# Half of q's projection ahead of the transposes of B's powers, q's convolution between the two rotations, and k's projection unsplit

## The chip, the cores and the metric

One core of a Trainium2 chip runs the whole kernel. The metric is the device time of one launch in microseconds, the median of the runs shown. A chance of "faster" or "slower" means by more than 0.3%.

## The reference

One layer of a decoder over 256 positions of width 1024, in float32. Cut to what matters here:

```python
h = rmsnorm(x, norm_mix_g)
p = h @ w_in            # [q | k | v | o (512 each) | i,f gates (4 each) | u (512)]
q, k = silu(conv4(q)), silu(conv4(k))          # causal, depthwise, 4 taps
A = sigmoid(o) * headnorm(mlstm(q, k, v, i, f))     # 4 heads of 128
s_t = a * s_(t-1) + Bbar u_t                   # S5: 32 groups of 16 channels, 64 complex states each
y = gelu(Re(C s) + D u);  z = y @ glu_w + glu_b;  B = z[:16] * sigmoid(z[16:])
x = x + concat([A, B]) @ w_out
x = x + top-1 of 4 expert groups, then top-2 of 8 SwiGLU experts (1024 -> 512 -> 1024) in it
return rmsnorm(x, norm_final_g)
```

## The kernel before

The program is one hand-written order of instructions for five in-order engines. There is no scheduler: what stands earlier in the code is issued earlier on its engine, and an instruction that waits holds everything behind it on that engine. SP is the queue of nearly all loads, and it is in order too.

**Memory.** `half(i)` is one of 23 buffers of 128 x 2048 float32 (1 MB each). They hold in turn the columns of w_in, temporaries, the split weights, w_out and at last the experts' weights. All 32 experts are streamed as 192 tiles of 1 MB; `fetch(upto)` issues tiles up to that number, and tile n goes into buffer `RO[n % 23]`. A tile's load waits until the last use of its buffer is over. Tiles 21 and 22 go into the buffers of `x1` (the residual) and of `xn`, which are free only when the parts of x for the experts have been made (lines 930 to 936).

**Front part, in the order of the code.** x is squared and transposed (L253 to L264), h = `h32` is written scaled and transposed (L277). `proj32T` (L422) multiplies w_in's columns with h in float32 and leaves the result transposed: u first, in PSUM banks 0 and 1. DVE meanwhile makes the powers of the S5 decay and B times those powers (`powers`, L355 to L363). u is copied to `U4`, C's transposes to `CT` (L477), the gates to `Gt` (L479). `transposeB` (L492, L495) turns B's powers; `inputs_to_states` (L520, L522) fills PSUM banks 4 to 7; `kernelK` and `transposeK` make the short S5 kernel, which ends in PSUM bank 1 and is read there by DVE at L596. Line 543 spreads rho, lines 544 to 546 make the sine and cosine (POOL made the angles, L391), lines 550 to 560 the gates' running sums. Then DVE runs `rotate(0)`, the kernel's mask (L595 to L598) and `rotate(1)` (L576 to L592): multiply by a rotation, scan, rotate back, for the two halves of the states.

**q, v, k, o.** q (L422, banks 2 and 3) and v (`proj32N`, L430, banks 0 and 1) run in float32. q then goes through `conv` (ACT L529, DVE L533, ACT L536). k and o are multiplied as sums of rounded parts: `prep` rounds a piece of a weight on ACT (L411) and subtracts it on POOL or DVE (L412), h is split the same way into `hH` and `hL` (L617, L618), and `projT` (L441 to L443) or `projN` (L453 to L457) takes three products. k also needs banks 2 and 3, so it starts only when q's convolution has read them. `states_to_outputs` (L648), `logweights` (L670) and the rest of k are interleaved; `outputs_back` (L655) turns S5's output, o follows, then k's convolution, `scores` (L664), the product with w_out in eight split pieces (`outs`, L805), the merge of the heads, and the routing. The experts (L1002) come last, in 16 pairs of 12 tiles.

The wait on PSUM that the change turns on stands in these lines of the order before:

```python
    rotate(1)
    run(proj32T("q", 2))
...
    run(proj32N("v", (0, 1)))
...
    for g in pc:
        run(g)
    cv = conv(0, 2)
```

## Time and profile before

| | |
|---|---|
| median of 3 runs | 642.94 us (642.47 to 644.63) |
| the profiled execution | 642.52 us, span 640.8 us |
| PE busy | 595.2 us (93% of the span) |
| DVE, ACT, POOL busy | 224.3, 135.5, 68.5 us |
| DMA, all queues | 219.78 MB, mean 343 GB/s |
| chain that ended last | PE 47%, DMA 32%, DVE 13%, ACT 4% |

Busy time is not the limit by itself: the chain names, going back from the end, what each piece of work waited for. The share of DMA comes from the stream of the experts; the shares of DVE and ACT come from the first 155 us. So the front has to be read engine by engine in time, and the experts' part by the rate of the stream.

### The profile page before, as it was taken

The numbers are of one execution on the slowest core, as the hardware profiler recorded it, in microseconds if no ns is written. First come the engines' busy times: TensorE is split into PE (matmuls) and PEld (weight loads), VectorE is DVE, ScalarE is ACT, GpSimd is POOL, SyncE is SP. The second block draws the span as 40 slices with busy tenths as digits, with TensorE's granted clock in tenths as the row PEclk, the third lists the DMA queues.
The fourth block names the chain that finished last, engine by engine and source line by source line (L and its number), as shares of the span: only waits on it lengthen the run. The fifth ranks groups of instructions, "written<-read, shape, count | busy, mean of one in ns | idle before, by whom it ended". The sixth has DMA issues, their size and how long they took to land.

```text
span 640.8 us, 8016 instructions
## 1 busy us (share of the span) xinstructions
PE 595.2 (93%) x3198; PEld 322.0 (50%) x3198; DVE 224.3 (35%) x548; ACT 135.5 (21%) x240; POOL 68.5 (11%) x77
## 2 busy tenths in 40 slices
PE   7979919999999999999999999999998999899993
PEld 6778408877864353353354335335343533354242
DVE  7939972186444231221212023122120212121123
ACT  2391364571332101101010010010100001001023
POOL 6010427255100000000000000000000000000003
PEclk8999958999999999999999999999999999999998
DMA  7781036657938999999999999999999999999992
GB/s 214 214 254 45 0 137 258 263 210 295 418 148 358 420 419 419 420 419 421 419 419 419 418 419 420 418 420 420 419 420 418 421 419 419 419 418 420 419 338 80
DMA packets 51336, 219.78 MB, mean 343 GB/s; under 512 B 15236, under 2 KB 20448, under 8 KB 27232
## 3 DMA queue, kind: packets, MB, share of 16 engines
q1 hardware_dynamic: 50944, 218.69, 85.4%
q8 instruction: 27, 0.44, 0.3%
q10 hardware_dynamic: 352, 0.54, 0.2%
q14 instruction: 13, 0.11, 0.0%
HBM read 218.17 MB, written 1.05 MB: 342 GB/s over the span
## 4 chain that ended last, share of the span: by engine, by line
PE 47%; DMA 32%; DVE 13%; ACT 4%; issue 1%; POOL 1%; SPq 0%; POOLq 0%; ACTq 0%; DVEq 0%
PE psum L1002 30%; DMA half<-in_expert_w_gate_dram 12%; DMA half<-in_expert_w_down_dram 9%; DMA half<-in_expert_w_up_dram 9%; PE psum L975 4%; PE psum L1017 3%; PE psum L805 2%; DVE mw L533 2%; PE psum L951 1%; DMA xs<-in_x_dram 1%; PE psum L648 1%; PE psum L441 1%; DVE half L583 1%; DVE half L357 1%; PE psum L1125 1%
## 5 line engine op out<-in xcount | busy, mean ns | idle before, releaser
L1002 PE MATMUL psum<-half,mw 128*64 128x512 f32 x1504 | 338.3, 596 | 9.5 <-DMA half<-in_expert_w_up_dram 4.2
L1002 PEld LDWEIGHTS psum<-half,mw 128*64 128x64 f32 x1504 | 110.3, 137 | 217.9 <-issue 186.9
L1009 DVE SCALAR_TENSOR_TENSOR Y<-psum,cst,Y 128x512 fp32r<-128x512 f32 x28 | 21.0, 751 | 134.2 <-ACT Y L1008 134.2
L1111 DVE TENSOR_TENSOR mw<-mw,psum 128x512 f32<-128x512 f32 x16 | 11.0, 687 | 143.7 <-PE psum L1002 143.7
L1008 ACT ACTIVATE Y<-psum,cst 128x512 fp32r<-128x512 f32 x28 | 19.2, 687 | 191.2 <-PE psum L1002 125.8
L1148 POOL MEMSET mw<- 128x2 f32 x1 | 0.1, 100 | 435.0 <-PE psum L1125 435.0
L412 POOL TENSOR_TENSOR half<-half,half 128x1024 fp32r<-128x1024 f32 x13 | 36.2, 2800 | 58.3 <-ACT half L411 47.6
L975 PE MATMUL psum<-cst,xs 128*128 128x256 bf16 (+1 forms) x384 | 40.9, 267 | 0.0
L975 PEld LDWEIGHTS <-xs 128*128 128x128 bf16 x384 | 40.0, 144 | 0.0
L1017 PE MATMUL psum<-Y,Sc 128*128 128x512 f32 x112 | 33.7, 423 | 0.0
L1126 ACT COPY mw<-psum 128x512 f32<-128x512 f32 x15 | 8.8, 587 | 114.4 <-PE psum L1125 114.4
L422 PE MATMUL psum<-half,half 128*128 128x256 f32 x128 | 30.8, 406 | 1.0 <-DVE half L277 1.0
L1017 PEld LDWEIGHTS psum<-Y,Sc 128*128 128x128 f32 x112 | 18.8, 188 | 25.3 <-issue 22.7
L958 DVE TENSOR_TENSOR mw<-psum,cst 128x512 f32<-128x512 f32 x32 | 22.1, 692 | 21.9 <-PE psum L975 18.3
L422 PEld LDWEIGHTS psum<-half,half 128*128 128x128 f32 x128 | 26.2, 206 | 5.2 <-DVE half L277 1.2
L805 PE MATMUL psum<-half,half 128*128 128x512 f32 x96 | 24.0, 401 | 0.6 <-ACT half L833 0.6
L441 PE MATMUL psum<-half,half 128*128 128x256 f32 x32 | 10.6, 332 | 14.2 <-DVE mw L533 14.0
L1104 ACT ACTIVATE mw<-psum 128x512 f32<-128x512 f32 x16 | 9.6, 597 | 52.8 <-PE psum L1002 52.8
L805 PEld LDWEIGHTS psum<-half,half 128*128 128x128 f32 x96 | 17.6, 188 | 4.7 <-ACT half L833 0.8
L992 DVE TENSOR_REDUCE cst<-psum 128x1 f32<-128x256 f32 x16 | 6.8, 425 | 26.9 <-PE psum L990 26.9
L411 ACT CAST half<-half 128x1024 fp32r<-128x1024 f32 x16 | 15.9, 1047 | 1.5 <-POOL half L412 1.0
L983 DVE TENSOR_SCALAR mw<-cst 128x64 f32<-128x64 f32 x64 | 15.6, 310 | 0.0
(348 smaller groups left out, 566.6 us busy)
## 6 DMA issues: line engine op xcount, KB each, us to landing
half<-in_expert_w_gate_dram SPq DMA_DIRECT2D x64, 1024.0 KB, 19.9
half<-in_expert_w_up_dram SPq DMA_DIRECT2D x64, 1024.0 KB, 19.9
half<-in_expert_w_down_dram SPq DMA_DIRECT2D x60, 1024.0 KB, 19.9
half<-in_w_in_dram SPq DMA_DIRECT2D x8, 1024.0 KB, 8.4
half<-in_w_out_dram SPq DMA_DIRECT2D x4, 1024.0 KB, 7.2
half<-in_expert_w_down_dram SPq DMA_DIRECT2D x6, 512.0 KB, 13.7
half<-in_w_in_dram SPq DMA_DIRECT2D x4, 512.0 KB, 7.3
xs<-in_x_dram SPq DMA_DIRECT2D x2, 512.0 KB
```

The costliest lines, as they stand in the source:

```text
L411: A.copy(made[i], w)
L412: es[i].tensor_tensor(rests[i], w, made[i].bitcast(F32), OP.subtract)
L422: MM(PS[:, bk + m // 2, 256 * (m % 2):256 * (m % 2) + 256], w[:, at:at + 128], flat(h32, c), start=c == 0 and m % 2 == 0, stop=c == 7, ski ...
L441: MM(o, wh[:, ms], flat(hH, c), start=c == 0 and m % 2 == 0, stop=False, skip_group_check=True)
L805: MM(PS[:, WB[2 * b + i], :], m[:, k % 4, ts], w[:, 512 * i:512 * i + 512], start=False, stop=n == 7 and m is ml, skip_group_check=True)
L958: TT(xg[:, cs, ss], PS[:, bk, :].rearrange("p (c s) -> p c s", c=n), fr(g2[:, cs], (1, n), (0, m)), OP.mult)
L975: MM(PS[:, DN[f % 2], m * c:m * c + m], xp[:, k, b, n * f + c::8], oh[:, b].rearrange("p e s -> p (e s)")[:, ss], start=c == b == k == 0, ...
L983: TS(ow[:, b, e], places, rk[:, b, 2 * pr + e:2 * pr + e + 1], wt[:, b, 2 * pr + e:2 * pr + e + 1], OP.is_equal, OP.mult)
L1002: MM(PS[64 * e:64 * e + 64, bk, 0:w[e].shape[-1]], lhs[:, c, 64 * e:64 * e + 64], w[e], start=c == 0, stop=c == n - 1, skip_group_check=True)
L1008: ACT(hi, src, AF.Copy, scale=w)
L1009: STT(lo, src, w, hi.bitcast(F32), OP.mult, OP.subtract)
L1017: MM(PS[:, WB[2 * b + n], :], Sc[:, b], Y[:, k], start=False, stop=False, skip_group_check=True)
```

## The change

Seven things change, all of them in order or in buffers except the second:

1. q's projection is a generator `qs`: four of its eight steps (16 products) run before `transposeB`, one between the two kernel transposes, three after. `conv(0, 2)` with its 12 DVE steps stands between `rotate(0)` and `rotate(1)`.
2. k is multiplied in float32 as q is (`proj32T("k", 2)`, 32 products) instead of in three rounded products; its four `prep` pieces are gone, `pieces` begins with o, and `projT` is gone.
3. h is rounded (`hH`) on ACT beside the first parameters, and `hL` is subtracted on POOL right behind the angles.
4. rho, the R rows and, ahead of B's copies, sine and cosine move earlier on ACT. In `transposeB` ACT takes one of four copies instead of two.
5. v's copy and C's powers follow v directly; the powers' temporaries move from buffers 21 and 17 to 0 and 1.
6. The loads of o and w_out move forward, `fetch` calls move back, and `RO` has a new order with buffer 22 for `xn` in place of 3.
7. The second half of x is loaded by ACT's queue, first of all; x's first square stands first on DVE; five small matmuls (`ident` with `ident`) stand between the transposes of x and u's projection.

The order table, the loads and the early part:

```diff
-    RO = (19, 17, 14, 16, 18, 11, 10, 20, 15, 22, 7, 21, 12, 2, 6, 0, 8, 1, 9, 4, 13, 5, 3)
+    RO = (14, 16, 18, 11, 10, 4, 19, 15, 7, 17, 20, 21, 12, 8, 1, 6, 0, 2, 3, 9, 13, 5, 22)
...
+    A.dma_start(xs[:, 1, :], xv[1])
...
-    SP.dma_start(xs[:, 1, :], xv[1])
...
+    STT(scr[:, 0, :], xs[:, 0, :], 1.0 / D, xs[:, 0, :], OP.mult, OP.mult, accum_out=ssq[:, 0:1])
+    V.tensor_copy(ldt0[0:16], rowsA[0:16, 0:2])
+    V.tensor_copy(rowsA[0:16, :].rearrange("p (g n) -> p g n", g=2), fr(ldt0[0:16], (1, 2), (0, 64)))
+    for b in range(2):
...
+        for c in range(8):
+            TR(xT[c][:, 128 * b:128 * b + 128], xs[:, b, c::8], ident)
...
+    for _ in range(2):
+        MM(PS[:, 0, 0:128], ident, ident, start=True, stop=True)
...
+    for _ in range(3):
+        MM(PS[:, 0, 0:128], ident, ident, start=True, stop=True)
...
+    hH, hL = [cuts(half(4 + i, F32R), (8, 2, 128))[0] for i in range(2)]
...
+    ACT(rho, b64(p["rho4"]), AF.Copy)
+    ACT(R[32:36], fr(dlt4[32:36], (0, 2), (1, 4), (0, 128)), AF.Copy)
...
+    for q in range(2):
+        A.copy(hH[:, 4 * q:4 * q + 4], h32[:, 4 * q:4 * q + 4])
...
-    t10, t11 = cuts(half(4), (4, 16, 16), (4, 16, 16))
+    t10, t11 = cuts(half(7), (4, 16, 16), (4, 16, 16))
...
-    pieces = [(g, i) for g in "ko" for i in range(4)] + [("w", k) for k in (4, 5, 6, 7, 0, 1, 2, 3)]
-    ROUNDED = (0, 2, 8, 20, 2, 6, 8, 9)
-    RESTS = (1, 3, 22, 9, 3, 0, 1, 4)
+    pieces = [(g, i) for g in "o" for i in range(4)] + [("w", k) for k in (4, 5, 6, 7, 0, 1, 2, 3)]
+    ROUNDED = (2, 9, 8, 1, 0, 3)
+    RESTS = (3, 19, 22, 6, 2, 9)
...
-    def projT(g, bk, i):
-        wh, wl = ready[g, i]
-        for cc in range(2):
-            c = 2 * i + cc
-            for m in range(4):
-                o = PS[:, bk + m // 2, 256 * (m % 2):256 * (m % 2) + 256]
-                ms = slice(512 * cc + 128 * m, 512 * cc + 128 * m + 128)
-                MM(o, wh[:, ms], flat(hH, c), start=c == 0 and m % 2 == 0, stop=False, skip_group_check=True)
-                MM(o, wh[:, ms], flat(hL, c), start=False, stop=False, skip_group_check=True)
-                MM(o, wl[:, ms], flat(hH, c), start=False, stop=c == 7, skip_group_check=True)
-                yield
...
+    qs = proj32T("q", 2)
...
+    for q in range(2):
+        cs = slice(4 * q, 4 * q + 4)
+        G.tensor_tensor(hL[:, cs], h32[:, cs], hH[:, cs].bitcast(F32), OP.subtract)
...
-            (A.copy if t % 2 else V.tensor_copy)(dst[:, 4 * t:4 * t + 4, :], src)
+            (A.copy if t == 3 else V.tensor_copy)(dst[:, 4 * t:4 * t + 4, :], src)
...
-    for i in range(2):
-        run(transposeB(i))
-    run(inputs_to_states())
...
-    ACT(rho, b64(p["rho4"]), AF.Copy)
...
+    STT(Bc[0:4], Gt[0:4], -1.0, Gt[0:4], OP.mult, OP.max)
+    for _ in range(4):
+        next(qs)
...
-    fetch(1)
...
+    load_w("o", (19, 21))
+    for i in range(2):
+        run(transposeB(i))
+    run(inputs_to_states())
...
+    next(qs)
     run(transposeK())
+    run(qs)
...
-    rotate(1)
-    run(proj32T("q", 2))
-    for j, a, b, n in ((0, 0, 96, 32), (1, 0, 64, 64), (2, 0, 32, 32), (2, 32, 64, 32), (2, 64, 96, 32), (3, 0, 0, 128)):
-        A.copy(Tz[b:b + n, :, j], KX[a:a + n])
-
-    run(proj32N("v", (0, 1)))
-    Cp = Bp
-    t10, t11 = cuts(half(17), (4, 16, 16), (4, 16, 16))
-    pc = [powers(V, Cp[0], CT, 1, True, 0, t00, t01), powers(V, Cp[1], CT, 1, True, 1, t10, t11)]
-    prep(2)
-    for g in pc:
-        run(g)
     cv = conv(0, 2)
     qk = cuts(half(7), (8, 256))[0]
     next(cv)
-    hH, hL = [cuts(half(4 + i, F32R), (8, 2, 128))[0] for i in range(2)]
-    for q in range(2):
-        cs = slice(4 * q, 4 * q + 4)
-        A.copy(hH[:, cs], h32[:, cs])
-        G.tensor_tensor(hL[:, cs], h32[:, cs], hH[:, cs].bitcast(F32), OP.subtract)
-    prep(4)
-    fetch(3)
+    for j, a, b, n in ((0, 0, 96, 32), (1, 0, 64, 64), (2, 0, 32, 32), (2, 32, 64, 32), (2, 64, 96, 32), (3, 0, 0, 128)):
+        A.copy(Tz[b:b + n, :, j], KX[a:a + n])
     for _ in range(4):
         next(cv)
-    V.memset(va[:, :, :, 128:129], 1.0)
+    prep(2)
+    rotate(1)
     next(cv)
+
+    run(proj32N("v", (0, 1)))
+    load_wo(4, 6)
     for b in range(2):
         A.copy(va[:, b, :, 0:128], PS[:, b, :].rearrange("p (h t) -> p h t", h=4))
-    load_w("o", (9, 6))
+    Cp = Bp
+    t00, t01 = cuts(half(0), (4, 16, 16), (4, 16, 16))
+    t10, t11 = cuts(half(1), (4, 16, 16), (4, 16, 16))
+    pc = [powers(V, Cp[0], CT, 1, True, 0, t00, t01), powers(V, Cp[1], CT, 1, True, 1, t10, t11)]
+    for g in pc:
+        run(g)
+    fetch(1)
+    load_wo(6, 0)
+    load_wo(2, 17)
+    prep(4)
...
+    run(proj32T("k", 2))
+    load_wo(0, 20)
+    states_to_outputs(0)
+    fetch(3)
...
-        run(projT("k", 2, i))
         logweights(i)
-        if i == 0:
-            states_to_outputs(0)
         TT(Em[:, i], PS[:, DB[i], :].rearrange("p (h t) -> p h t", h=4), fr(cap, (0, 4), (1, 128)), OP.min)
-    fetch(5)
...
-    fetch(7)
+    fetch(5)
...
-    for i in range(2, 4):
-        run(projT("k", 2, i))
...
-    load_wo(4, 0)
-    load_wo(6, 1)
...
-            prep(10)
...
-    load_wo(0, 4)
-    load_wo(2, 22)
...
+    fetch(8)
+    run(scores())
     fetch(9)
-    run(scores())
     for i in range(3):
         STT(Em[:, i], PS[:, (6, 4, 2)[i], :].rearrange("p (h t) -> p h t", h=4), 128.0 ** -0.5, Em[:, i], OP.mult, OP.mult)
+    prep(10, (G, V))
...
-    prep(14, (G, V))
-    prep(16, (G, V))
...
-    xn = cuts(half(3), (2, 1024))[0]
+    xn = cuts(half(22), (2, 1024))[0]
```

**PE, from u's projection to the first S5 output.** Buffers `half_5`, `half_6` are q's columns, `half_7`, `half_8` v's; `half_9`, `half_10` hold B's powers; `half_27`, `half_28` (before) are k's rounded parts and rests, `half_14`, `half_15` (after) k itself. In the order before, left of the S5 rows L520, L522 and L503:

```order
L463 MATMUL psum<-half_12_146,half_2_73 36x256 x8
L466 MATMUL psum<-ident,half_2_73 128x128 x8
L492 MATMUL psum<-ident,half_9_125 128x128 x16
L492 MATMUL psum<-ident,half_10_126 128x128 x16
...
L563 MATMUL psum<-ident,half_1_72 128x76
L512 MATMUL psum<-ident,mw 128x128 x4
L422 MATMUL psum<-half_12_146,half_5_104 128x256 x16
L422 MATMUL psum<-half_12_146,half_6_106 128x256 x16
L430 MATMUL psum<-half_7_118,half_12_146 128x512 x8
L430 MATMUL psum<-half_8_120,half_12_146 128x512 x8
L441 MATMUL psum<-half_30_631,half_27_610 128x256
L442 MATMUL psum<-half_31_632,half_27_610 128x256
```

And in the order of the change:

```order
L463 MATMUL psum<-ident,half_2_73 128x128 x8
L430 MATMUL psum<-half_12_144,half_5_104 128x256 x16
L491 MATMUL psum<-ident,half_9_125 128x128 x16
L491 MATMUL psum<-ident,half_10_126 128x128 x16
...
L430 MATMUL psum<-half_12_144,half_6_106 128x256 x4
L511 MATMUL psum<-ident,mw 128x128 x4
L430 MATMUL psum<-half_12_144,half_6_106 128x256 x12
L438 MATMUL psum<-half_7_118,half_12_144 128x512 x8
L438 MATMUL psum<-half_8_120,half_12_144 128x512 x8
L430 MATMUL psum<-half_12_144,half_14_212 128x256 x16
L430 MATMUL psum<-half_12_144,half_15_214 128x256 x16
L647 MATMUL psum<-half_13_204,half_18_220 64x128 x16
```

Half of q has moved ahead of the transposes of B's powers, and 32 products of k stand in a row where 96 rounded ones were spread among the S5 products.

**ACT, from the gates to the running sums.** `half_1_72` holds CT, `half_2_73` the gates. Before:

```order
L477 COPY half_1_72<-psum 64x256 x4
L479 ACTIVATE half_2_73<-psum,cst 36x256
L480 ACTIVATE mw<-cst 4x1024
L495 COPY half_21_385<-psum 128x512 x2
L495 COPY half_22_386<-psum 128x512 x2
L543 ACTIVATE half_20_286<-half_2_73 128x1024
L544 ACTIVATE half_19_285<-half_18_284 128x1024
L545 ACTIVATE half_18_284<-half_18_284 128x1024
L546 ACTIVATE half_19_285<-half_18_284,cst 128x1024
L551 ACT_TABLE_LOAD
```

In the change:

```order
L477 COPY half_1_72<-psum 64x256 x4
L479 ACTIVATE half_2_73<-psum,cst 36x256
L542 ACTIVATE half_22_297<-half_21_296 128x1024
L543 ACTIVATE half_21_296<-half_21_296 128x1024
L544 ACTIVATE half_22_297<-half_21_296,cst 128x1024
L494 COPY half_23_397<-psum 128x512
L494 COPY half_24_398<-psum 128x512
L551 ACT_TABLE_LOAD
```

The R rows and rho are gone from here, two copies have gone to DVE, and sine and cosine stand ahead of the copies.

**SP, behind k's columns.** In the change (`half_25`, `half_26` are o's columns, w_out's pieces are 4, 6, 2, 0 in this order):

```order
L173 DMA half_25_421<-in_w_in_dram 128x4x512
L173 DMA half_26_423<-in_w_in_dram 128x4x512
L180 DMA half_32_649<-in_w_out_dram 128x2x1024
L147 DMA half_35_665<-in_expert_w_gate_dram 128x2048
L180 DMA half_36_667<-in_w_out_dram 128x2x1024
L180 DMA half_37_669<-in_w_out_dram 128x2x1024
L180 DMA half_41_716<-in_w_out_dram 128x2x1024
L147 DMA half_42_734<-in_expert_w_gate_dram 128x2048
L147 DMA half_43_736<-in_expert_w_gate_dram 128x2048
L147 DMA half_46_789<-in_expert_w_gate_dram 128x2048
L147 DMA half_47_791<-in_expert_w_up_dram 128x2048
```

Before, three tiles of the experts stood ahead of o's columns and seven ahead of w_out; now one tile does.

## Rows read from the trace of the kernel before

**Rows 1.** windows of the late part: us, busy by engine (instructions), PEclk, DMA share, GB/s

```profile
118.00:153.00 35.00, 35.00 (x227) 28.43 (x226) 22.24 (x53) 19.85 (x41) 15.66 (x9) 1.00 0.56 214
...
184.00:195.00 11.00, 11.00 (x54) 3.82 (x55) 8.39 (x24) 8.45 (x14) 0.00 (x0) 1.00 0.29 96
...
195.00:614.00 419.00, 407.90 (x2050) 178.08 (x2046) 89.35 (x230) 38.56 (x61) 0.10 (x1) 1.00 1.01 418
```

**Rows 2.** timeline of DVE around the first experts: start, us, what

```profile
192.32 2.42 DVE L936 TENSOR_TENSOR xs<-half,xs 128x1024 bf16<-128x1024 f32 x2
```

**Rows 3.** PE's waits from 93 to 185 us: total, times, longest

```profile
PE psum L441 <- DVE mw L533: 14.0, 1, 14.0
...
PE psum L805 <- ACT half L833: 0.6, 1, 0.6
...
PE psum L829 <- DVE mw L794: 0.4, 1, 0.4
```

**Rows 4.** timeline of PE up to 120 us: start, us, what, [idle before]

```profile
12.17 16.84 PE L422 MATMUL psum<-half,half 128*128 128x256 f32 x64 [1.04 <-DVE half L277]
...
36.45 2.70 PE L492 MATMUL psum<-ident,half 128*128 128x128 f32 x20 [2.84 <-ACT half L477]
...
40.68 0.33 PE L520 MATMUL psum<-half,half 128*128 128x64 f32 x2
...
51.48 13.98 PE L422 MATMUL psum<-half,half 128*128 128x256 f32 x64
...
65.30 13.90 PE L430 MATMUL psum<-half,half 128*128 128x512 f32 x32
...
108.93 1.12 PE L670 MATMUL psum<-mw 36*128 36x512 f32 x2
...
110.19 1.97 PE L648 MATMUL psum<-half,half 128*64 128x128 f32 x32
...
118.03 1.95 PE L655 MATMUL psum<-ident,half 128*32 128x128 f32 x64
```

**Rows 5.** chain that ended last, up to 130 us: start, us, what

```profile
1.74 6.37 DMA xs<-in_x_dram
...
37.10 0.47 ACT half L479
...
41.49 1.06 ACT half L543
...
45.63 1.28 ACT L551
...
52.72 1.21 DVE mw L560
...
64.00 0.67 DVE half L596
```

**Rows 6.** timeline of POOL and DVE: two users of SBUF side by side

```profile
33.32 1.04 POOL L391 TENSOR_TENSOR half<-half,half 128x512 int32<-128x512 int32 x1
...
37.17 0.69 DVE L495 COPY half<-psum 128x512 f32<-128x512 f32 x1 [2.32 <-ACT half L477]
...
92.04 4.69 POOL L618 TENSOR_TENSOR half<-half,half 128x1024 fp32r<-128x1024 f32 x2 [13.47 <-ACT half L617]
...
97.00 2.34 DVE L634 TENSOR_SCALAR cst<-cst 128x4 f32<-128x4 f32 x1
```

**Rows 7.** timeline of ACT ahead of the S5 output

```profile
99.36 1.99 ACT L411 CAST half<-half 128x1024 fp32r<-128x1024 f32 x2 [0.96 <-POOL half L412]
...
110.09 0.60 ACT L685 ACTIVATE half<-psum 128x512 f32<-128x512 f32 x1 [7.43 <-PE psum L670]
...
110.64 1.15 ACT L688 ACTIVATE half<-half 128x512 f32<-128x512 f32 x2
```

**Rows 8.** timeline of DVE in the heads' norm

```profile
147.92 1.55 DVE L781 SCALAR_TENSOR_TENSOR cst<-mw 128x4 f32<-128x4 f32 x1
```

**Rows 9.** window in which PE stood behind v's projection

```profile
79.20:82.80 3.60, 0.00 (x0) 0.00 (x0) 3.57 (x6) 0.00 (x0) 0.00 (x0) 0.98 0.00 0
```

More of the change, by code (lines that the diff above doesn't have):

```diff
@@ L251, in tile_hymba @@
     flat = lambda t, c: t[:, c].rearrange("p b t -> p (b t)")
-    for c in range(8):
-        TR(xT[c][:, 0:128], xs[:, 0, c::8], ident)
-    TR(PS[:, 4, 0:48], rowsA[0:48, :], ident[0:48, 0:48])
-    for c in range(8):
-        TR(xT[c][:, 128:256], xs[:, 1, c::8], ident)
-    STT(scr[:, 0, :], xs[:, 0, :], 1.0 / D, xs[:, 0, :], OP.mult, OP.mult, accum_out=ssq[:, 0:1])
-    V.tensor_copy(rT, PS[:, 4, 0:48])
-    ldt, lre, lim = rT[:, 0:16], rT[:, 16:32], rT[:, 32:48]
+    STT(scr[:, 0, :], xs[:, 0, :], 1.0 / D, xs[:, 0, :], OP.mult, OP.mult, accum_out=ssq[:, 0:1])
[4 more added lines that the diff above has]
+            TR(xT[c][:, 128 * b:128 * b + 128], xs[:, b, c::8], ident)
+    TR(PS[:, 4, 0:48], rowsA[0:48, :], ident[0:48, 0:48])
+    for _ in range(2):
+        MM(PS[:, 0, 0:128], ident, ident, start=True, stop=True)
     STT(scr[:, 0, 0:512], xs[:, 1, 0:512], 1.0 / D, xs[:, 1, 0:512], OP.mult, OP.mult, accum_out=sh[:, 1, 0:1])
@@ L267, in tile_hymba @@
                   "cr", "ci", "t1", "t2", "rho4"], [spar[:, i] for i in range(20)]))
+    V.tensor_copy(rT, PS[:, 4, 0:48])
+    ldt, lre, lim = rT[:, 0:16], rT[:, 16:32], rT[:, 32:48]
     ACT(p["dt"], ldt, AF.Exp)
@@ L311, in tile_hymba @@
     ACT(p["rho4"], p["lrdt"], AF.Exp, scale=4.0)
+    U4, rho = cuts(half(18), (16, 64), (16, 64))
+    b64 = lambda ap: fr(ap, (1, 16), (0, 64))
+    ACT(rho, b64(p["rho4"]), AF.Copy)
+    ACT(R[32:36], fr(dlt4[32:36], (0, 2), (1, 4), (0, 128)), AF.Copy)
     rnd(V, p["n"], p["th"], 1.0 / TWO_PI)
@@ L382, in tile_hymba @@
     cosT, sinT = cuts(half(17), (16, 64), (16, 64))
-    U4, rho = cuts(half(18), (16, 64), (16, 64))
-    b64 = lambda ap: fr(ap, (1, 16), (0, 64))
     ta = ta.bitcast(I32)
@@ L479, in tile_hymba @@
     ACT(Gt[0:36], PS[0:36, 4, 0:256], AF.Identity, bias=gbias[0:36, 0:1])
-    ACT(R[32:36], fr(dlt4[32:36], (0, 2), (1, 4), (0, 128)), AF.Copy)
     cw = rTB[:, 0:32].rearrange("p (w t) -> p w t", w=4)
@@ L562, in tile_hymba @@
     A.copy(K4T, PS[:, 0, :])
-    TR(PS[:, 3, 0:76], rowsB[0:76, :], ident[0:76, 0:76])
-    A.copy(rTB[:, 0:76], PS[:, 3, 0:76])
+    TR(PS[:, 1, 0:76], rowsB[0:76, :], ident[0:76, 0:76])
+    A.copy(rTB[:, 0:76], PS[:, 1, 0:76])
+    next(qs)
     run(transposeK())
+    run(qs)
     tt = cuts(half(12), (3, 8, 64))[0]
```

4 lines of the change are left out of this document (1 added, 3 removed).

## The prediction

> **What bounds the kernel now.** I read backwards. The windows of the late part come first [rows 1]: from 195 to 614 us DMA moves 418 GB/s, so one tile of 1 MB lands every 2.5 us, and PE's clock is 1.00 there. The stream of the experts sets the end. In the stretch just before, 184 to 195, the queue moves only 96 GB/s. The reader is to see why: the next tiles go into the buffers of `x1` and `xn`, and DVE's last reading of them ends at 192.32 + 2.42 = 194.7 [rows 2]. That reading hangs on the routing, and the routing on everything before it. So the end follows the front one to one, as long as the other 21 tiles lie in their buffers by then.
>
> The front is then read through PE's waits [rows 3] and PE's timeline [rows 4]. From 118 to 153 PE is busy in 35.00 of 35.00 us [rows 1]; after that there are only small waits, 0.6 and 0.4 us [rows 3]. Before it stands one large wait: k may start only when q's convolution has read banks 2 and 3, and PE stands 14.0 us for that [rows 3], from v's end at 79.20 to 93.2. The chain [rows 5] says what is late: u's outputs, the gates, the R rows, the running sums, then DVE with `rotate(0)` and the mask (L596). So up to 79 the bound is the ACT and DVE chain, then a PE that waits for DVE's queue order, then PE.
>
> **The change part by part**, against the profiled execution (642.52 us; the median of the runs lies 0.42 above it).
>
> *x and the warm-up.* x is asked for at 1.74 and lands 6.37 later [rows 5]. On ACT's queue the second half can go out up to 0.9 us sooner: a gain of 0.9 if the landing follows. But DVE's square of the first half now stands directly ahead of that of the second; at worst about 1.4 us, twice a 128x512 operation of 0.69 [rows 6], comes late. I take 0, and keep −0.9 and +1.4 for the range. A rule speaks against the gain: the Trainium skill, "DMA: Bandwidth & Descriptors", section "Issuing engines are not separate DMA queues", says that transfers run on the same 16 engines whoever issues them, and another issuer saves only issue time. By it this term is between 0 and +1.4, without it down to −0.9; the first trace shows no x on ACT's queue, so it is open here. The five small matmuls stand where PE waits. u's 64 products took 16.84, q's same 64 took 13.98 [rows 4]; the difference, 2.86, is one spell at the low clock level (1.2 of 2.4 GHz). I take it that the five keep the clock up, so u ends 2.9 earlier; otherwise see the second rival.
>
> *Half of q in the gap.* Before B's transposes PE stood 2.84 us behind ACT's L477 [rows 4]. Half of q, 13.98 / 2 = 7.0, fills this gap and the 2.9 that u has won. The cover is that DVE isn't ready sooner. `hL` on POOL follows the angles (33.32 + 1.04 = 34.4) and lasts 4.7 for both halves, to 39.1 [rows 6]. DVE operations of a kind of `nci` (128x4) took 2.34 beside POOL [rows 6], so I let `nci` end with POOL and the copies of B begin at 39.8. Behind it on DVE wait six copies, 0.69 each [rows 6]: 39.8 + 6 x 0.69 = 43.95. PE's first S5 product, at 40.68 before [rows 4], waits for these: 3.3 later.
>
> *ACT's chain.* The gates end at 37.10 + 0.47 [rows 5]. Sine and cosine took 42.55 to 45.63, 3.1; now they follow at once, to 40.7. Two spreads of 1.06 (L543 is one) left the chain. ACT's last copy ends near 43.5; then table, running sums and last gate step take what they took, 45.63 to 52.72 + 1.21 = 53.93, 8.3 [rows 5]. `rotate(0)` so starts at 51.8, 2.1 sooner, and the mask's last read of bank 1 ends at 64.67 − 2.1 = 62.55.
>
> *v and k.* From 40.68 to q's end at 51.48 + 13.98 = 65.46 PE needed 24.8 with all of q [rows 4]; 7.0 of it now lies earlier, so 17.8, and q ends at 61.7. v's first product (13.90 / 16 = 0.87 for a pair of banks) then meets the freed bank 1 at 62.6: no wait, v ends at 75.6. q's convolution stands right behind the mask on DVE and is over near 70, so k's banks are free before v ends. k follows without a pause: 13.98 [rows 4] to 89.6. **This is the 14.0 us wait**, gone. What the 96 split products cost need not be priced: the sum goes from clock time to clock time. What is late next? On SP the first load of w_out (`load_wo(4, 6)`) goes into a buffer of v's and stands until 75.6, with all of SP behind it: tile 0, the rest of w_out, the next tiles. Their first users come at about 98. On DVE, rotation and C's powers now stand between mask and S5's outputs. All that DVE did from 64.67 to k's start at 93.2 is 28.6; begun at 62.55 it ends by 91.1. Only the third S5 product needs the last of it.
>
> *To S5's output.* Behind k come two S5 products, 1.97 each, and three `logweights`, 1.12 each [rows 4]: the third ends at 89.6 + 3.94 + 3.36 = 96.9. PE's third S5 product ends at 99.1. The tail is now ACT's: a table (1.28 as at L551 [rows 5]), the Exps (110.09 to 111.79, 1.7), the two roundings of w_out that stand ahead of the copy (1.99), and the copy (0.60, as the other 128x512 read from PSUM) [rows 7]: 5.6, so `outputs_back` starts at 102.5 instead of 118.03 [rows 4]: **−15.5**.
>
> *Behind it.* The order on PE stays, o and k's convolution as before. Two late pairs of `prep` with POOL's subtractions move; the heads' norm (1.55 for a 128x4 operation [rows 8], where an undisturbed one is far below 0.69) and the waits of 0.6 and 0.4 [rows 3] should lose together about **0.9** (bounds 0 and −2.4).
>
> *Loads.* SP now issues o's and w_out's loads ahead of all but one tile, 25 loads in all until the tiles are in place. At 2.5 us each they need 62; from 75 to the experts' new start near 168 there are 93. I price this at nothing; the cover is this slack of 30 us.
>
> Sum: 0 − 15.5 − 0.9 = −16.4, so 642.52 − 16.4 = 626.1 on the profile's footing, 626.5 against the median. The bounds of the terms (x −0.9 to +1.4, late waits −1.5 to +0.9, and some 2 us in the tail, if POOL delays nothing or ACT's roundings run behind their loads) make 622.5 to 630 for this case. A measurement of this kernel can tell about 0.3%, 1.9 us, from no change.
>
> **The rivals.**
>
> 1. *The clock falls in front of `outputs_back`.* PE has nothing from 99.1 to 102.5. In a window of 3.60 us without PE work the mean clock was still 0.98 [rows 9], and the gap of 2.84 was followed by full speed, while 14.0 was not; 3.4 lies near the first two. If it falls, a spell like u's costs 2.86: 629.4. Chance 0.17.
> 2. *The five matmuls don't do what they are there for.* u's clock is low as before (16.84). Then half of q ends 2.9 later, the transposes of B feed DVE late, its copies end about 1.5 later, and everything behind them with it: 628. For it: PE still waits for DVE's parts of h in front of u, 1.04 [rows 4]. Against it: these waits are short. Chance 0.25.
> 3. *The stream doesn't follow.* In 184 to 195 the queue was idle for (418 − 96) / 418 x 11 = 8.5 us [rows 1]. If the 21 tiles are in place only just in time, since the fetches stand behind w_out's pieces on SP, no more than about these 8.5 are won: 634.4. Against it the slack of 30 us. Chance 0.07.
> 4. *Slower.* The clock falls in the same place as in the first rival, and the many short waits in the stretch behind (roundings on ACT, subtractions on POOL now nearer to their use) keep it at the low level. Every microsecond there does half its work, so it costs half: the gain of 16.4 is gone when the low level lasts 33 us, and if it lasts 66, as long as the way to the experts, the price is 33: 659. Against it: 118 to 153 was busy in every microsecond and the clock 1.00 [rows 1]. Chance 0.04.
>
> **How the numbers follow.** Forecast 0.43, rivals 0.25, 0.17, 0.07 and 0.04; 0.04 for an unseen wait of the size of the gain. The first three cases all lie between 622 and 631, and the third rival needs 634 at most half way, so 622 to 633 leaves out well under 2 in 10. Slower takes the last rival and part of the unseen: 0.05; within 0.3% the rest of the unseen and a stream that follows little: 0.04; faster 0.91.
>
> **What would show it.** Right: sine directly behind the gates; `rotate(0)` at about 51.8; the first S5 product near 44; v's products without a wait, from 61.7; k from 75.6 to 89.6 in one piece; `outputs_back` at 102.5 with ACT's copy as its releaser; the experts' first products near 168 and the queue at 418 GB/s from about 178 on. Wrong: a wait of PE of over 2 us in front of v or k; a mean clock of 0.5 behind 102; the S5 products waiting on DVE's powers of C; or a queue that is idle after 178, which would mean that a tile, not the routing, comes last.

## The result

The change makes the kernel faster: 627.46 us median (625.27 to 628.37, 4 runs) against 643.21 (642.47 to 644.63) before, a ratio of 0.9748 with a 95% interval of 0.9715 to 0.978. The forecast was 626.5, in a range of 622 to 633. The profiled execution took 628.37 us with a span of 626.4, the longest of the four.

PE's timeline after the change, to be held against [rows 4]: start, us, what, idle before.

```profile
11.53 14.08 PE L430 MATMUL psum<-half,half 128*128 128x256 f32 x64 [0.37 <-DVE half L280]
...
30.04 7.07 PE L430 MATMUL psum<-half,half 128*128 128x256 f32 x32
...
39.76 2.20 PE L491 MATMUL psum<-ident,half 128*128 128x128 f32 x16 [0.90 <-DVE half L494]
...
61.69 13.14 PE L438 MATMUL psum<-half,half 128*128 128x512 f32 x30 [1.48 <-DVE half L598]
74.67 13.98 PE L430 MATMUL psum<-half,half 128*128 128x256 f32 x64
...
94.28 1.12 PE L669 MATMUL psum<-mw 36*128 36x512 f32 x2
...
95.55 1.97 PE L647 MATMUL psum<-half,half 128*64 128x128 f32 x32
100.90 3.64 PE L654 MATMUL psum<-ident,half 128*32 128x128 f32 x64 [3.38 <-ACT half L700]
...
158.98 4.20 PE L943 MATMUL psum<-mw,half 128*128 128x128 f32 x16
...
169.73 13.95 PE L994 MATMUL psum<-half,mw 128*64 128x512 f32 x64
```

k (74.67) follows v without a pause; the 14.0 us of [rows 3] are gone. In their place stand 1.48 us ahead of v's second product and 3.38 ahead of `outputs_back` (L654). And the products of L654, which turn S5's output (32 in the code; each stands as two in the row's x64), take 3.64 where they took 1.95 [rows 4].

Windows after the change, as in [rows 1]: us, busy by engine, granted clock, DMA share, GB/s.

```profile
98.00:108.00 10.00, 7.10 (x75) 5.84 (x76) 0.26 (x1) 7.27 (x13) 8.77 (x5) 0.66 1.02 419
...
160.00:168.00 8.00, 8.00 (x36) 8.00 (x37) 2.46 (x13) 0.00 (x0) 0.00 (x0) 0.57 0.61 255
166.00:176.00 10.00, 10.00 (x49) 5.90 (x50) 5.33 (x19) 4.20 (x10) 0.00 (x0) 0.90 0.02 7
182.00:614.00 432.00, 420.76 (x2148) 185.41 (x2146) 93.33 (x231) 43.14 (x72) 1.96 (x4) 1.00 1.01 413
```

Two stretches have a low granted clock: 98 to 108 (mean 0.66) and 160 to 168 (0.57). The queue is all but empty from 166 to 176 (7 GB/s) and moves 413 GB/s from 182 on: the tiles lay in their buffers in time, and the stream again waits only for the last reading of `x1` and `xn`, which ends at 177.94 + 2.42 = 180.36 below.

DVE's timeline at three places (start, us, what): the operation ahead of B's copies and the copies, the heads' norm that [rows 8] showed at 1.55, and the last reading of [rows 2]. The first took 2.06 where it took 0.28 before (at 41.05 there); POOL's work on h lies beside it. The norm's operation is down to 0.17.

```profile
36.47 2.06 DVE L538 TENSOR_SCALAR half<-half 128x256 f32<-128x256 f32 x1 [2.25 <-ACT half L477]
...
38.92 3.68 DVE L494 COPY half<-psum 128x512 f32<-128x512 f32 x6
...
133.09 0.17 DVE L773 SCALAR_TENSOR_TENSOR cst<-mw 128x4 f32<-128x4 f32 x1
...
177.94 2.42 DVE L928 TENSOR_TENSOR xs<-half,xs 128x1024 bf16<-128x1024 f32 x2
```

The chain that ended last, front part (start, us, what), against [rows 5]:

```profile
0.82 4.68 DMA xs<-in_x_dram
...
49.68 1.21 DVE mw L560
...
60.97 0.68 DVE half L598
61.69 13.14 PE psum L438 x30
...
98.48 1.88 ACT half L419 x2
100.36 0.49 ACT half L700
100.90 3.64 PE psum L654 x64
```

From 61.69 to 95.4 the chain is PE alone. Then it is ACT: table, exponentials, the two roundings of w_out (L419), the copy (L700).

| place (us in the span) | before | predicted | after |
|---|---|---|---|
| `rotate(0)` | 53.9 | 51.8 | 50.8 |
| first S5 product | 40.7 | near 44 | 41.8 |
| q ended | 65.5 | 61.7 | 59.4 |
| mask has read bank 1 | 64.7 | 62.55 | 61.6 |
| k starts | 93.2 | 75.6 | 74.7 |
| third `logweights` ended | 110.05 | 96.9 | 95.4 |
| `outputs_back` | 118.0 | 102.5 | 100.9 |
| experts' first product | 184.1 | near 168 | 169.7 |
| end | 640.8 | 624.4 | 626.4 |

From the experts' first product to the end both executions take 456.7 us: the end followed the front one to one. The front up to `outputs_back` won 17.1 instead of 15.5; the stretch from there to the experts lost 2.7 (68.8 us instead of 66.1) where 0.9 was to be won. These are readings of the profiled execution, the longest of the four.

### The profile page after: what moved, and what is told of

It reads as the page before. It is cut to its first block, busy times and chain, and to the rows that moved or that the text cites. A ratio compares the mean times of both kernels' runs of the same rounds, so it can differ in the third digit from the quotient of the medians.

```text
span 626.4 us, 7955 instructions
## 1 busy us (share of the span) xinstructions
PE 595.8 (95%) x3176; PEld 321.8 (51%) x3176; DVE 218.1 (35%) x549; ACT 130.7 (21%) x234; POOL 57.9 (9%) x74
## 4 chain that ended last, share of the span: by engine, by line
PE 56%; DMA 36%; DVE 3%; ACT 2%; issue 1%; POOL 1%; POOLq 0%; SPq 0%; DVEq 0%; ACTq 0%
PE psum L994 28%; DMA half<-in_expert_w_down_dram 13%; DMA half<-in_expert_w_up_dram 13%; DMA half<-in_expert_w_gate_dram 10%; PE psum L430 6%; PE psum L797 4%; PE psum L967 3%; PE psum L1009 2%; PE psum L438 2%; PE psum L943 1%; PE psum L1117 1%; DMA xs<-in_x_dram 1%; PE psum L449 1%; PE psum L1013 1%; PE psum L451 1%; PE psum L453 1%
## 5 line engine op out<-in xcount | busy, mean ns | idle before, releaser
L430 PEld LDWEIGHTS psum<-half,half 128*128 128x128 f32 x192 | 36.2, 190 | 5.7 <-DVE half L280 0.6
L420 POOL TENSOR_TENSOR half<-half,half 128x1024 fp32r<-128x1024 f32 x10 | 24.5, 2469 | 64.6 <-ACT half L419 46.8
L797 PE MATMUL psum<-half,half 128*128 128x512 f32 x96 | 24.2, 402 | 0.3 <-ACT half L825 0.3
L797 PEld LDWEIGHTS psum<-half,half 128*128 128x128 f32 x96 | 17.5, 188 | 4.6 <-ACT half L825 0.5
L438 PE MATMUL psum<-half,half 128*128 128x512 f32 x32 | 14.2, 596 | 1.5 <-DVE half L598 1.5
L1117 PE MATMUL psum<-ident,mw 128*128 128x128 f32 x64 | 10.7, 290 | 1.7 <-DVE mw L1103 1.7
```

Source lines behind the costliest of these rows:

```text
L420: es[i].tensor_tensor(rests[i], w, made[i].bitcast(F32), OP.subtract)
L430: MM(PS[:, bk + m // 2, 256 * (m % 2):256 * (m % 2) + 256], w[:, at:at + 128], flat(h32, c), start=c == 0 and m % 2 == 0, stop=c == 7, ski ...
L438: MM(PS[:, bks[b], :], h32[:, c, b], raw[g, c // 2][:, 512 * (c % 2):512 * (c % 2) + 512], start=c == 0, stop=c == 7, skip_group_check=True)
L797: MM(PS[:, WB[2 * b + i], :], m[:, k % 4, ts], w[:, 512 * i:512 * i + 512], start=False, stop=n == 7 and m is ml, skip_group_check=True)
L1117: TR(PS[:, GB, 128 * c:128 * c + 128], act[:, c::4], ident)
```

## The experiments

Times are medians; each kernel was run beside the kernel before on its chip, and the ratio is to that. The changed kernel's own ratio is 0.9748 [0.9715, 0.978], so a difference from it of under 2 us is told by the traces rather than by the medians. ACT's new order, the powers' new buffers and the order of the loads (parts 4 to 6 of the change) were not taken back apart; what they give is read from rows alone.

### q's convolution put back behind the powers

```diff
-    for _ in range(4):
-        next(cv)
     prep(2)
     rotate(1)
-    next(cv)
...
     for g in pc:
         run(g)
+    run(cv)
```

> The changed kernel with q's convolution (its 12 DVE steps and its last ACT step) put back behind the second rotation and C's powers; everything else stays. Theory A, the place of q's convolution on DVE is what released k: DVE reaches the convolution about 18.7 us later (the second rotation and the powers took 68.57 to 87.3), so k starts near 87.4 instead of 74.67, PE stands about 12.7 us between v and k, its clock falls there (a spell costs 2.9), and the end moves by 12.7 to 15.6: 640 to 643 us, nearly the whole gain gone. Theory B, k in float32 (no rounded pieces, no waiting for them) is what brought the gain: under 3 us, at most 631.

Measured: 643.53 us, ratio 0.9998 [0.9986, 1.0011], 0.5 above theory A's range. The whole gain is gone. Its PE timeline:

```profile
64.16 13.90 PE L438 MATMUL psum<-half,half 128*128 128x512 f32 x32
87.01 2.04 PE L430 MATMUL psum<-half,half 128*128 128x256 f32 x4 [8.95 <-ACT half L373]
89.91 14.89 PE L430 MATMUL psum<-half,half 128*128 128x256 f32 x60 [0.85 <-DVE mw L532]
```

k starts at 87.01, 0.4 from what theory A said. The trace names ACT for the wait, but bank 2 was read by the first six of DVE's twelve convolution steps (12 steps take 5.79 from 83.97), which end at 86.9. The wait is 8.95 and not 12.7, because v ended at 78.06 instead of 74.83: the clock was low from 44 to 55 (mean 0.57). k then takes 17.8 instead of 13.98, its first part at the low clock. The later start, 12.3, and the longer k, 3.8, are the 16.1 us of the medians. So without the convolution's new place nothing of the change's gain is left. That does not yet say that the new place is enough.

### The convolution's new place alone, in the kernel before

```diff
-    rotate(1)
     run(proj32T("q", 2))
+    cv = conv(0, 2)
+    qk = cuts(half(7), (8, 256))[0]
+    next(cv)
     for j, a, b, n in ((0, 0, 96, 32), (1, 0, 64, 64), (2, 0, 32, 32), (2, 32, 64, 32), (2, 64, 96, 32), (3, 0, 0, 128)):
         A.copy(Tz[b:b + n, :, j], KX[a:a + n])
+    for _ in range(4):
+        next(cv)
...
+    prep(4)
+    rotate(1)
+    next(cv)
```

(hH and hL are made ahead of that `prep(4)`, v's copy directly behind v. So the split of h and of k's pieces, which stood behind the second rotation but for two pieces, moves ahead of it together with the convolution; the convolution alone, with these left behind, was not run.)

> The kernel before with one part of the change alone: q's convolution, the rounding and splitting of h and of k's pieces stand between the mask and the second rotation, v's copy directly behind v; k is still three rounded products, q whole and late, all else as before. Theory A, the place of the convolution on DVE is what freed k: the 14.0 us wait and the clock spell behind it shrink to under 3, and the end is 10 to 15 us sooner than before, 628 to 633. Rival, k in float32 is needed as well: POOL's subtractions of h and of k's pieces, 14 us in a row, now come after the convolution and PE waits for them, or they slow DVE's second rotation so that ACT's rounding for o comes late, as with the split k in the changed kernel; 635 or more.

Measured: 646.78 us, ratio 1.0049 [1.0034, 1.0065], 0.5% slower than before. The timelines of its DVE and of its POOL, and the list of PE's waits (total, times, longest):

```profile
74.10 2.84 DVE L580 TENSOR_TENSOR half<-half 128x512 f32<-128x512 f32 x1
...
79.63 6.67 DVE L583 TENSOR_TENSOR_SCAN half<-half,half 128x512 f32<-128x512 f32 x2
```

```profile
76.36 12.13 POOL L412 TENSOR_TENSOR half<-half,half 128x1024 fp32r<-128x1024 f32 x4
```

```profile
PE psum L647 <- ACT half L363: 9.1, 1, 9.1
PE psum L654 <- ACT half L700: 6.1, 1, 6.1
```

The 14.0 us wait is gone here too. But POOL now subtracts h and k's four pieces beside the second rotation, and the two scans take 6.67 (2.33 in the changed kernel, at 73.52). C's powers come so late that the second S5 product stands 9.1 us, and `outputs_back` starts at 119.42, 1.4 later than before. Of the two theories the rival holds. ACT also waited 10.27 us for o's columns. They stand on SP behind a tile of the experts, and SP stood 53.6 us with that tile until DVE's last step of C's powers (L357) was over, so this wait too follows the slow rotation; it wasn't tried apart.

### k split again, in the changed kernel

```diff
-    pieces = [(g, i) for g in "o" for i in range(4)] + [("w", k) for k in (4, 5, 6, 7, 0, 1, 2, 3)]
+    pieces = [(g, i) for g in "ko" for i in range(4)] + [("w", k) for k in (4, 5, 6, 7, 0, 1, 2, 3)]
...
-    prep(2)
+    prep(4)
     rotate(1)
...
-    run(proj32T("k", 2))
+    for i in range(4):
+        run(projT("k", 2, i))
```

> The changed kernel with k multiplied again as three products of rounded parts: its four pieces are rounded on ACT and subtracted on POOL behind q's convolution, o's first two pieces follow later, two w_out loads move behind k, C's powers use two other temporaries. Theory A: k's 96 products take 11.5 us instead of 13.98, but o's pieces now stand on ACT ahead of the table and the exponentials, so the output of S5 starts between 1 us sooner and 2 us later; the end is at 626 to 630 us and no wait of over 3 us appears ahead of k. Theory B: the rounded pieces are what k waited for; PE waits for POOL's subtractions ahead of or in k, 5 to 14 us, 633 to 642.

Measured: 636.41 us, ratio 0.9878 [0.986, 0.9896], 9 us more than the changed kernel. No wait ahead of k, as theory A had it; but A's end is missed by 6 to 10. The time lies in theory B's range, yet the wait that B named isn't there: the place is another. The list of PE's waits, then the timelines of ACT and of POOL:

```profile
PE psum L664 <- ACT half L713: 12.9, 1, 12.9
```

```profile
95.39 5.78 ACT L419 CAST half<-half 128x1024 fp32r<-128x1024 f32 x6
...
105.92 0.60 ACT L697 ACTIVATE half<-psum 128x512 f32<-128x512 f32 x1 [3.46 <-POOL half L420]
```

```profile
96.51 9.38 POOL L420 TENSOR_TENSOR half<-half,half 128x1024 fp32r<-128x1024 f32 x4 [16.53 <-ACT half L419]
```

k's products end at 88.2, in the changed kernel at 88.6 (k takes 2 us less, and started 1.5 later). What is lost is behind: ACT's six roundings in a row and POOL's four subtractions stand ahead of the exponentials, and `outputs_back` waits 12.9 instead of 3.38. The exponentials wait for POOL because they are written into buffer 21 (`Em`), which holds o's columns until POOL has subtracted them. So k in float32 costs PE some 2 us and takes four roundings and four subtractions from ACT and POOL at the place where these two come to bound the kernel. Against the kernel before, this kernel with a split k is still 1.2% faster: 7 of the 16 us are won without k in float32.

### All of q's projection late again

```diff
-    for _ in range(4):
-        next(qs)
...
-    next(qs)
     run(transposeK())
     run(qs)
```

> The changed kernel with all of q's projection behind the S5 kernel's last transpose again (no half ahead of B's transposes, no step between the kernel's transposes). Theory A: the half of q, 7.0 us, lay in a gap in which PE only waited for DVE and ACT; put back it lies on PE's path. The S5 products start no more than 1 us sooner, v's wait of 1.5 for the mask goes, so k starts 4.5 to 5.5 later and the end is at 631 to 633 us. Rival: the gap was not free, B's transposes start 7 sooner without it and the S5 part with them, and the end stays within 1.5 of the changed kernel.

Measured: 632.82 us, ratio 0.9831 [0.9812, 0.9849], 5.4 more than the changed kernel, as theory A said.

```profile
36.10 3.47 PE L491 MATMUL psum<-ident,half 128*128 128x128 f32 x16 [5.61 <-ACT half L477]
...
80.88 13.98 PE L430 MATMUL psum<-half,half 128*128 128x256 f32 x64
```

PE stands 5.61 us where the half of q had been, and B's transposes start only 0.85 sooner. k starts 6.2 later, more than the 4.5 to 5.5 that A named: u started 0.3 later in this execution, and after the pause the clock was low, so that the first transposes of B took 3.47 instead of 1.91. v has no wait here. By the medians, half of q is worth about what it takes (7.07), less the 1.48 that v waits with it.

### The five small matmuls left out

```diff
-    for _ in range(2):
-        MM(PS[:, 0, 0:128], ident, ident, start=True, stop=True)
...
-    for _ in range(3):
-        MM(PS[:, 0, 0:128], ident, ident, start=True, stop=True)
```

> The changed kernel without the five small matmuls ahead of u's projection. Theory A: they keep PE's clock up; without them u's 64 products take about 16.8 instead of 14.08 with a granted clock of 0.5 over some 5 us, half of q ends 2.8 later, B's copies on DVE start some 1.6 later and the rest moves by that: 629 to 630 us. Rival: the landing of x and its 16 transposes in a row already keep the clock up; u stays at 14.1 and the end at 627.5.

Measured: 627.44 us, ratio 0.9755 [0.9724, 0.9786]: no difference that can be told. The end is the rival's. In the trace they do what theory A said, for less:

```profile
12.04 15.77 PE L426 MATMUL psum<-half,half 128*128 128x256 f32 x64 [1.04 <-DVE half L276]
```

u takes 15.77 instead of 14.08, with a mean clock of 0.79 from 10 to 18 us instead of 1.00. Of the 2.2 us by which u ends later, 0.9 reach k (75.54). This profile had no second low stretch (experts at 168.50), and the 0.9 is no more than what that stretch comes and goes with. u took 16.84 in the kernel before: so the five matmuls account for 1.69 of the 2.76 that u became shorter. The other 1.07 came without them; x's 16 transposes stand in one row now, but that was not tried apart.

### x on one queue

```diff
-    A.dma_start(xs[:, 1, :], xv[1])
...
     SP.dma_start(xs[:, 0, :], xv[0])
+    SP.dma_start(xs[:, 1, :], xv[1])
```

> The changed kernel with both halves of x asked for by SP again, one behind the other. Theory A, another issuer saves issue time alone (0.4 us for one issue): u starts 0.4 to 0.7 later than at 11.53 and the end moves by that, 627.9 to 628.2. Rival: the issue on another queue lets the second half land some 2 us sooner (the chain of the changed kernel has x landing at 5.5, that of before at 8.1); put back, u starts 1.5 to 2.5 later and the end is at 629 to 630.

Measured: 625.74 us, ratio 0.9723 [0.9704, 0.9742]. The 1.7 us less are within the medians' uncertainty, but the trace shows that both theories had the sign wrong. When each half lands shows in the squares, which wait for it (DVE for the first half, ACT for the second; this kernel, then the changed one):

```profile
4.52 1.23 DVE L250 SCALAR_TENSOR_TENSOR half<-xs 128x1024 f32<-128x1024 f32 x1 [1.96 <-DMA xs<-in_x_dram]
...
5.94 0.63 ACT L260 ACTIVATE half<-xs 128x512 f32<-128x512 f32 x1 [2.44 <-DMA xs<-in_x_dram]
```

```profile
5.52 1.23 DVE L250 SCALAR_TENSOR_TENSOR half<-xs 128x1024 f32<-128x1024 f32 x1 [2.96 <-DMA xs<-in_x_dram]
...
5.75 0.63 ACT L260 ACTIVATE half<-xs 128x512 f32<-128x512 f32 x1 [1.76 <-DMA xs<-in_x_dram]
```

On two queues both halves land together, at 5.5 and 5.75. On one, back to back, the second comes 0.2 later, but the first 1.0 sooner, and its square is the long one. u starts at 10.85 instead of 11.53. The other kernels bear it out: u starts at 10.78 to 10.87 in the four profiles with both halves on SP (this kernel and the combinations below), and at 11.53 to 13.45 in the seven with x on two queues and the five matmuls. The other 1 us lies in shorter low stretches (0.77, 0.50 and 0.87 in the windows of 2 us from 100 to 106) and isn't shown to be x's doing. In the kernel before, x's second half was late (8.1) because the load of `lambda` stood between the halves, not because both were on SP: on SP and ACT, this kernel asks for the same loads first, in another order at this place alone, and the half lands at 5.9. The rule weighed in the prediction (the Trainium skill, "DMA: Bandwidth & Descriptors", section "Issuing engines are not separate DMA queues") is that transfers run on the same 16 engines whoever issues them. The trace agrees: the second queue shortened nothing, and the halves, asked for together, landed together.

### PE kept busy ahead of `outputs_back`

```diff
     states_to_outputs(2)
+    for _ in range(13):
+        MM(PS[:, 7, 128:256], ident, ident, start=True, stop=True)
```

> The changed kernel with 13 small products of the identity (some 3.1 us) on PE behind the third S5 product, in the 3.38 us in which PE waits for ACT's copy; nothing else. Theory A, that wait lowers the clock: the output's transposes take 1.95 instead of 3.64, o's first products go at full speed, no row below 1.00 between 98 and 110, and the end is 2.5 to 3 us sooner, 624.5 to 625. Rival: the clock falls there for another reason, as in 160 to 168, where PE was busy; the low rows stay and the end is at 627.5.

Measured: 624.74 us, ratio 0.9707 [0.9693, 0.9721]; 2.7 less than the changed kernel, as theory A said (13 products, x26 in the row).

```profile
97.53 3.17 PE L693 MATMUL psum<-ident 128*128 128x128 f32 x26
100.93 1.96 PE L654 MATMUL psum<-ident,half 128*32 128x128 f32 x64 [0.23 <-ACT half L702]
```

`outputs_back` starts no sooner and takes 1.96. From its start to the experts it is 66.2 us, 2.6 less; the low stretch near 160 is still there. So the wait itself lowers the clock there, and that costs 2.6.

### Two roundings moved behind the Gelus

```diff
-    prep(8)
...
     outputs_back()
+    prep(8)
     cv = conv(1, 2)
```

> The changed kernel with the two roundings of w_out's pieces 6 and 7 on ACT moved from ahead of S5's output copy to behind the four Gelus. Theory A: the output's transposes start 2.0 us sooner, at 98.9, the wait shrinks from 3.38 to 1.4 and the clock stays up, which gives 2.9 more: 622.5 to 623.5 us. Rival: the roundings now hold up ACT's first step of k's convolution and w_out's products; 0 to 1 us gained, 626.5 or more.

Measured: 622.68 us, ratio 0.9678 [0.9665, 0.9691]; 4.8 less, as theory A said.

```profile
100.81 1.95 PE L654 MATMUL psum<-ident,half 128*32 128x128 f32 x64 [1.49 <-ACT half L699]
...
156.30 4.07 PE L943 MATMUL psum<-mw,half 128*128 128x128 f32 x16
...
166.18 13.95 PE L994 MATMUL psum<-half,mw 128*64 128x512 f32 x64
```

In this execution u started 1.8 later than in the changed kernel's, so 100.81 stands for 99.0. The wait is 1.49 and no window of 2 us to 190 has a low clock. From `outputs_back` to the experts it is 65.37 us: 0.7 less than before the change, which is the small late gain that had been forecast at 0.9. The roundings' new place has no part in it: up to L943 it is 55.49 us here and 55.47 in the kernel with the filled wait, where they stand as in the change. From L943 to the experts it is 9.88 us here, 9.90 before the change and 10.75 in the changed kernel, so the low stretch there costs 0.87.

### The rest of h later on POOL

```diff
     angles()
-    for q in range(2):
-        cs = slice(4 * q, 4 * q + 4)
-        G.tensor_tensor(hL[:, cs], h32[:, cs], hH[:, cs].bitcast(F32), OP.subtract)
...
     prep(2)
+    for q in range(2):
+        cs = slice(4 * q, 4 * q + 4)
+        G.tensor_tensor(hL[:, cs], h32[:, cs], hH[:, cs].bitcast(F32), OP.subtract)
     rotate(1)
```

> The changed kernel with POOL's two subtractions that make the rest of h moved behind q's convolution (they are used only by o). Theory A, POOL beside DVE holds up the operation ahead of B's copies (L538, 2.06 us for 128x256): without it that takes under 0.7, the copies of B start some 1.3 us sooner, the S5 chain 1.0 us sooner, and the end is at 626.2 to 627. Rival: the copies wait for PE's transposes anyway, or the two subtractions hold up the second rotation instead and that reaches S5's products; 627.5 or more.

Measured: 629.1 us, ratio 0.9788 [0.9769, 0.9807], as the rival said; 1.6 more than the changed kernel.

```profile
36.48 0.29 DVE L535 TENSOR_SCALAR half<-half 128x256 f32<-128x256 f32 x1 [2.27 <-ACT half L474]
...
37.59 3.68 DVE L491 COPY half<-psum 128x512 f32<-128x512 f32 x6 [0.16 <-PE psum L488]
...
74.92 4.48 DVE L582 TENSOR_TENSOR_SCAN half<-half,half 128x512 f32<-128x512 f32 x2
...
102.86 3.64 PE L654 MATMUL psum<-ident,half 128*32 128x128 f32 x64 [6.09 <-ACT half L700]
```

POOL had indeed held up the one operation: 0.29 instead of 2.06, the copies 1.3 sooner, k 0.75 sooner. But now it holds up the second rotation (scans 4.48 instead of 2.33), C's powers and ACT's work behind them come 3.5 later, and `outputs_back` 2 us later.

### Combinations

`prep(8)` late and x on SP:

```diff
-    A.dma_start(xs[:, 1, :], xv[1])
...
+    SP.dma_start(xs[:, 1, :], xv[1])
...
-    prep(8)
...
     outputs_back()
+    prep(8)
```

> The changed kernel with the roundings of w_out's pieces 6 and 7 behind the Gelus and both halves of x on SP, back to back. If both gains add (4.8 and 1.7 us were measured apart, of which 0.7 is the earlier start of u and the rest is the low clock, which the first edit has already removed): 621.5 to 622.3 us. If x's place gives nothing on top: 622.7.

Measured: 622.3 us, ratio 0.9671 [0.9657, 0.9685]. That is 0.4 less than with the late roundings alone (622.68), which the medians can't tell from nothing; u starts at 10.80. Then, on top, S5's output copy ahead of two exponentials:

```diff
-    for i in range(2):
-        ACT(Em[:, i], Em[:, i], AF.Exp)
...
     for h in range(2):
         (V.tensor_copy if h else A.copy)(YT[:, h], PS[:, h, :].rearrange("p (q f) -> p q f", q=4))
+    for i in range(2):
+        ACT(Em[:, i], Em[:, i], AF.Exp)
     outputs_back()
```

> As the one before, and S5's output copy on ACT also ahead of the two last exponentials (1.15 us). The wait ahead of the output's transposes, 1.49 with the roundings moved, shrinks to about 0.4, and the end is 1 us sooner than with the two edits, about 620.9. Rival: the exponentials now hold up the Gelus and the table, and o's glu products with them; no gain.

Measured: 621.96 us, ratio 0.9655 [0.9639, 0.967]; the wait is 0.46, `outputs_back` 0.97 sooner than with two edits (97.30 against 98.27). In time 0.3 of it shows, less than the runs differ by. It has the lowest median here, 5.5 us below the changed kernel. And on top, the rest of h on POOL behind `prep(4)`, with `gbd` ahead of `prep(6)`:

```diff
     prep(4)
+    for q in range(2):
+        cs = slice(4 * q, 4 * q + 4)
+        G.tensor_tensor(hL[:, cs], h32[:, cs], hH[:, cs].bitcast(F32), OP.subtract)
...
+    for k in range(2):
+        G.tensor_tensor(gbd[:, :, k], fr(gw0[:, :, 16 * k:16 * k + 16], (32, 4), (0, 8), (1, 16)),
+                        fr(mask8, (0, 4), (1, 8), (0, 16)), OP.mult)
     prep(6)
```

> As the one before, and POOL's rest of h moved behind o's first four pieces, where DVE has little to do, with the glu weights' masks ahead of w_out's first pieces. The operation ahead of B's copies takes 0.29 instead of 2.06, k starts 0.75 sooner as it did with the rest of h behind the convolution, the second rotation is not held up, and the end is 0.7 sooner, about 620.2. Rival: o waits for the rest of h on POOL; 621 or more.

(The same lines go from their old places.) Measured: 623.98 us, ratio 0.9699 [0.9686, 0.9713]: 2 more, as the rival said, but not for its reason: o's first products start no later behind `outputs_back`.

```profile
60.17 14.84 PE L438 MATMUL psum<-half,half 128*128 128x512 f32 x30 [2.05 <-DVE half L595]
```

q is ready 1.4 sooner but the mask only 0.8, so v's second product waits 2.05 instead of 1.47, and v then runs at a low clock from 61 to 65: 14.84 instead of 13.14. k starts 0.9 later than without the edit. A second loss lies behind: POOL's work is 4.7 us longer, so its subtractions for w_out (100.56 to 110.3) now meet DVE's gating of S5's output. One product of it takes 2.01 instead of 0.43, and DVE starts k's convolution 2.8 later (111.74 instead of 108.98).

## Why the prediction held

**The wait ahead of k: right, and shown.** k was to start at 75.6 and start it did at 74.67. That the convolution's place does it is shown by its removal (k at 87.01, ratio 0.9998). What the prediction did not say is what the place costs where POOL's subtractions stand beside the second rotation: in the kernel before, moved together with the split of h and k, it wins nothing (1.0049). The prediction counted k's freed pieces only as "need not be priced"; they are worth 9 us of the 16, since the changed kernel with a split k wins 7.

**The early terms: right in mechanism, 1 us too small.** u started 0.64 sooner where 0 was taken (bounds −0.9 and +1.4), and ACT's queue has no part in that: with both halves on SP it is 1.32. u itself became 2.76 shorter, as forecast (2.9), but only 1.69 of it is the five matmuls'. B's copies started at 38.92, not 39.8, since POOL began and ended 0.7 sooner. (`nci` is 128x256, not 128x4; it did end with POOL, as assumed.) The first S5 product came at 41.79 and not near 44: it did not wait for all six copies, which end at 42.60. So q ended at 59.4, not 61.7, and v's second product, which was to have no wait, stood 1.48 for the mask. The half of q took the 7.0 us counted for it (5.4 by the medians when taken away). From k to `outputs_back`, the table's 1.6 us too much are 0.9 from ahead of k and 0.6 from adding up rows that overlap: from k's start to the end of the third `logweights` it is 20.7, not 21.3, since two `logweights` in a row take 1.91 up to the next product, not twice 1.12.

**The wait ahead of `outputs_back`: right to 0.02** (3.4 predicted, 3.38 measured) **and wrong in what follows.** The step that failed is the likeliest case's assumption that the clock stays up there; the first rival (0.17) came about at its place, with 2.6 to 2.7 us for the 2.86 that it named. The argument from [rows 9] was weak: the mean of 0.98 hides that the clock began to fall within that window of the kernel before.

```profile
82.00:83.00 1.00, 0.00 (x0) 0.00 (x0) 0.97 (x2) 0.00 (x0) 0.00 (x0) 0.82 0.00 0
83.00:84.00 1.00, 0.00 (x0) 0.00 (x0) 1.00 (x2) 0.57 (x1) 0.00 (x0) 0.50 0.00 0
```

**Behind it: 0.7 instead of 0.9, and a low stretch that nobody had in the sum.** 160 to 168 costs 0.87 (L943 to the experts, 10.75 with it and 9.88 without). Put together: −17.1 + 2.6 + 0.87 − 0.7 = −14.3, and the spans differ by 14.4. In the profiled execution a front 1.6 better and a clock 3.5 worse partly cancel, so that the span is 2.0 longer than forecast; the median lies 0.9 below this execution. That the forecast of 626.5 is only 1 us from the median is in part luck.

**The loads and the stream: right.** The queue is idle ahead of 176 and at full rate from 182. The second and third rivals didn't come about (u takes 14.08; the end follows one to one), nor the fourth: the two low stretches lasted some 7 us each. Its price, half of every microsecond at the low level, is too high here: they cost 2.6 and 0.87.

## What to carry to other kernels

When an in-order engine has to free a PSUM bank, put that reading ahead of longer work that nobody waits for yet, and look in the same breath at who shares the time it moves into; here it paid in full only together with taking POOL's work away. After a change that removes a long wait, look for short waits that remain in front of PE: filling 3.4 us, or moving 2 us of roundings out of them, gave another 2.7 and 4.8 us. Here, splitting a load over two queues delayed the half that was wanted first: ask which half the front waits for.
